# Multiply and tanh-GELU on one core: three DRAM stretches and two load queues, against two stretches and one

## The chip, the cores and the metric

The kernel runs on one core of a Trainium2 chip. The metric is device time in microseconds (us); the kernel before takes 119.77 us, the median of 3 runs that lie between 119.68 and 119.78.

A core has five instruction engines. Three matter here: VectorE (DVE in the profile) multiplies, ScalarE (ACT) applies the GELU, and SyncE (SP) issues DMAs and waits. Sixteen DMA engines carry all data between DRAM and the on-chip memory (SBUF, 128 partitions). A DMA becomes packets, here one packet for each row of a partition; the trace keeps a record of every packet with its queue, start, duration and size. Queue q1 is fed by SP, queue q10 by ACT.

## The reference

```python
def setup_inputs():
    batch, dim = 1024, 4096
    return {
        "x": np.random.randn(batch, dim).astype(np.float32),
        "y": np.random.randn(batch, dim).astype(np.float32),
    }

def reference(x, y):
    z = x * y
    return (0.5 * z * (1 + np.tanh(np.sqrt(2 / np.pi) * (z + 0.044715 * z ** 3)))).astype(np.float32)
```

Every element stands alone: 16.78 MB of x, 16.78 MB of y in, 16.78 MB out. Which element lies in which partition is therefore free, as long as x, y and the output agree.

## The kernel before, in words

The 4,194,304 elements are seen as 128 partitions of 32768 columns. `PIECES` (line 14) cuts the columns in three pieces: 1280, 16384 and 15104 columns. Each piece is one contiguous stretch of DRAM, and inside it partition p owns one contiguous row (`columns`, lines 51 to 55). The rows are 5120, 65536 and 60416 bytes long, and so are the packets. A DMA over 128 rows gives each of the 16 DMA engines 8 packets.

x has a place for all 32768 columns in SBUF (`xs`); the product and the GELU overwrite it, and the stores read it. y has a smaller buffer (`ys`, 20440 columns), so the second part of y can only be loaded when products have freed the room. `Y_LOADS` (line 16) lists y's loads as (first column, end, place in the buffer), and `Y_FREE` (line 18) how many products must be done before each is issued. The loads of y go in the order: middle piece (16384 columns), last piece (15104), first piece (1280).

The order of work is written out by hand:

- Two loads are hoisted ahead of the start-up barrier (`_hoist`): x's 1280-column piece on SP (line 79) and x's 16384-column piece on ACT (line 80). These two queues share the DMA engines at the opening.
- SP waits until the small piece of x has landed (line 81), then issues y's first load (line 82, issued by line 75) and x's last piece (line 83, issued by line 71).
- SP then waits for 3 products and issues y's second load, waits for the fourth and issues y's third (lines 84 to 87).
- DVE multiplies in steps (`STEPS`, line 20: four of 4096 columns; seven of 2048 and one of 768; one of 1280), each after the waits of lines 95 and 96. ACT follows each product with a GELU (line 107) after the wait of line 106.
- SP stores in three DMAs (lines 112 to 116): the middle piece after y's second load has fully landed (line 114), though its GELUs are done long before; then the last piece; then the small one. SP waits for the first two stores, clears the semaphores and waits for the third (lines 117 to 122).

All of SP's DMAs are on one queue, and on each DMA engine its packets go in the order in which they were issued.

Of the kernel before, what the change touches and what calls it, by code (L numbers as in the profile page):

```python
# [1 line left out]

# [4 lines left out]


F32 = mybir.dt.float32
GELU = mybir.ActivationFunctionType.Gelu_apprx_tanh  # L10

PIECES = [(0, 1280), (1280, 17664), (17664, 32768)]

Y_LOADS = [(1280, 17664, 4056), (17664, 32768, 0), (0, 1280, 15104)]

Y_FREE = [0, 3, 4]

STEPS = [[4096] * 4, [2048] * 7 + [768], [1280]]  # L20
STORES = [(1280, 17664), (17664, 32768), (0, 1280)]
Y_BUF = 20440


def _hoist(nc, issued):

    here = nc.cur_bb.bb.instructions
    first = nc.main_func.blocks[0].instructions
    for ins in issued:
        del here[next(k for k, i in enumerate(here) if i is ins or i.name == ins.name)]  # L30
    engine = issued[0].engine
    at = next(
        k
        for k, i in enumerate(first)
        if i.engine == engine and type(i).__name__ == "InstDrain"
    )
    first[at:at] = issued


@with_exitstack  # L40
def kernel(
    ctx: ExitStack,
    tc: tile.TileContext,
    x: bass.AP,
    y: bass.AP,
    out: bass.AP,
):
    nc = tc.nc
    P = nc.NUM_PARTITIONS

    def columns(t, a, b):

        flat = t.flatten_outer_dims().rearrange("r c -> (r c)")
        pa, pb = next(q for q in PIECES if q[0] <= a and b <= q[1])
        return flat[P * pa : P * pb].rearrange("(p c) -> p c", p=P)[:, a - pa : b - pa]


    tc.close()
    tc.compile()

    xs = nc.alloc_sbuf_tensor("xs", [P, PIECES[-1][1]], F32).ap()
    ys = nc.alloc_sbuf_tensor("ys", [P, Y_BUF], F32).ap()
    sem_x = [nc.alloc_semaphore(f"sem_x{i}") for i in range(len(PIECES))]
    sem_y = [nc.alloc_semaphore(f"sem_y{i}") for i in range(len(Y_LOADS))]
    sem_mul = nc.alloc_semaphore("sem_mul")
    sem_act = nc.alloc_semaphore("sem_act")
    sem_o = [nc.alloc_semaphore(f"sem_o{i}") for i in range(len(STORES))]

    def load_x(i, engine=nc.sync):
        a, b = PIECES[i]  # L70
        return engine.dma_start(out=xs[:, a:b], in_=columns(x, a, b)).then_inc(sem_x[i], 16)

    def load_y(i):
        a, b, r = Y_LOADS[i]
        return nc.sync.dma_start(
            out=ys[:, r : r + b - a], in_=columns(y, a, b)
        ).then_inc(sem_y[i], 16)

    _hoist(nc, [load_x(0).ins])
    _hoist(nc, [load_x(1, nc.scalar).ins])  # L80
    nc.sync.wait_ge(sem_x[0], 16)
    load_y(0)
    load_x(2)
    for i in range(1, len(Y_LOADS)):
        if Y_FREE[i]:
            nc.sync.wait_ge(sem_mul, Y_FREE[i])
        load_y(i)

    nc.scalar.wait_ge(sem_x[0], 16)
    n = 0  # L90
    done = {}
    for i, (a, b, r) in enumerate(Y_LOADS):
        for j, (xa, xb) in enumerate(PIECES):
            if xa <= a < xb:
                nc.vector.wait_ge(sem_x[j], 16)
        nc.vector.wait_ge(sem_y[i], 16)  # L96
        c = a
        for w in STEPS[i]:
            nc.vector.tensor_mul(  # L99
                out=xs[:, c : c + w],  # L100
                in0=xs[:, c : c + w],
                in1=ys[:, r + c - a : r + c - a + w],
            ).then_inc(sem_mul, 1)
            n += 1
            done[c + w] = n
            nc.scalar.wait_ge(sem_mul, n)
            nc.scalar.activation(  # L107
                out=xs[:, c : c + w], in_=xs[:, c : c + w], func=GELU
            ).then_inc(sem_act, 1)
            c += w  # L110

    for i, (a, b) in enumerate(STORES):
        if i == 0:
            nc.sync.wait_ge(sem_y[-2], 16)
        nc.sync.wait_ge(sem_act, done[b])
        nc.sync.dma_start(out=columns(out, a, b), in_=xs[:, a:b]).then_inc(sem_o[i], 16)
    for i in range(len(STORES) - 1):
        nc.sync.wait_ge(sem_o[i], 16)
    nums = sorted(s.num for s in [*sem_x, *sem_y, *sem_o[:-1], sem_mul, sem_act])
    assert nums == list(range(nums[0], nums[-1] + 1))  # L120
    nc.sync.sem_clear(range(nums[0], nums[-1] + 1))
    nc.sync.wait_ge(sem_o[-1], 16).then_inc(sem_o[-1], -16)


# [1 line left out]
_INS = ['x', 'y']  # L126
_OUTS = [((1024, 4096), 'float32')]


# [23 lines left out]
```

## Time and profile before

| what | value |
|---|---|
| runs of the kernel before | 119.68, 119.77, 119.78 us |
| profiled execution, first to last instruction (span) | 118.5 us |
| its first DMA packet starts, its last one ends | 1.01 us, 118.12 us |
| its last store has landed | 118.48 us |
| DVE busy, ACT busy | 35.2 us, 30.9 us |
| moved | 50.33 MB: 33.55 MB read, 16.78 MB written |

The profiled execution has no time of its own beside the span; the median of the runs stands 1.25 us above the span's 118.52 us. Times in the profile count from the first instruction, which is SP's hoisted DMA. "Busy" leaves out waits and DMA issues. "To landing" runs from a DMA's issue to the last increment of its semaphore; sixteen increments, one for each DMA engine, make a DMA complete.

### The profile page before, as it was taken

The page shows a single profiled execution, that of the slowest core. Times are in us where ns is not written, and L with a number is a line of the kernel's source. Part 1 is how long each engine was busy: PE and PEld are TensorE (multiplying, and loading weights), DVE is VectorE, ACT ScalarE, POOL GpSimd, SP SyncE. Part 2 cuts the span into 40 slices and gives each one's busy share as a digit, 9 for nine tenths or more (in the row PEclk, how much of TensorE's full clock was granted, in tenths as well). Part 3 has the DMA queues.
Part 4 walks back from the last instruction along what each step waited for, and adds up shares of the span by engine and source line. Part 5 has one row for each costly group of instructions (what it writes and reads, how often), then busy time and mean ns, then how long its engine had stood idle before and what let it go on. Part 6 is the DMA issues. An engine that isn't in the chain of part 4 may idle for free.

```text
span 118.5 us, 83 instructions
## 1 busy us (share of the span) xinstructions
DVE 35.2 (30%) x13; ACT 30.9 (26%) x14; POOL 0.2 (0%) x4
## 2 busy tenths in 40 slices
DVE  0000000000000069999920000059999940000000
ACT  0000000000000000999975000006998990000000
POOL 0000000000000000000000000000000000000000
DMA  9888899889988897798797797798899887977975
GB/s 492 382 382 382 354 597 464 354 354 465 597 354 354 354 632 347 326 632 347 326 632 347 326 632 347 326 575 354 354 531 531 354 354 326 653 326 326 653 326 221
DMA packets 1296, 50.33 MB, mean 425 GB/s; under 512 B 144, under 2 KB 144, under 8 KB 528
## 3 DMA queue, kind: packets, MB, share of 16 engines
q1 hardware_dynamic: 1152, 41.94, 82.3%
q10 hardware_dynamic: 144, 8.39, 16.5%
HBM read 33.55 MB, written 16.78 MB: 425 GB/s over the span
## 4 chain that ended last, share of the span: by engine, by line
DMA 55%; DVE 24%; ACT 3%; issue 1%; DVEq 0%
DMA ys<-in_y_dram 43%; DVE xs L99 24%; DMA xs<-in_x_dram 11%; ACT xs L107 3%; DVEq L96 0%
## 5 line engine op out<-in xcount | busy, mean ns | idle before, releaser
L99 DVE TENSOR_TENSOR xs<-xs,ys 128x2048 f32<-128x2048 f32 (+3 forms) x13 | 35.2, 2778 | 60.9 <-DMA ys<-in_y_dram 60.9
L107 ACT ACTIVATE xs<-xs 128x2048 f32<-128x2048 f32 (+3 forms) x13 | 29.6, 2300 | 19.6 <-DVE xs L99 19.6
L107 ACT ACT_TABLE_LOAD x1 | 1.3, 1283 | 47.2 <-DVE xs L99 47.2
L137 POOL MEMSET const-uint8-127<- 128x1 uint8 x1 | 0.1, 102 | 0.0
L137 POOL MEMSET const-bfloat16-1.0<- 128x1 bf16 x1 | 0.1, 101 | 0.0
L137 POOL MEMSET const-float32-0.0<- 128x1 f32 x1 | 0.1, 98 | 0.2 <-issue 0.2
L137 POOL MEMSET const-float32-1.0<- 128x1 f32 x1 | 0.1, 98 | 0.0
## 6 DMA issues: line engine op xcount, KB each, us to landing
xs<-in_x_dram SPq DMA_DIRECT2D x1, 7552.0 KB, 46.5
ys<-in_y_dram SPq DMA_DIRECT2D x1, 7552.0 KB, 22.5
out_dram<-xs SPq DMA_DIRECT2D x1, 7552.0 KB, 20.4
xs<-in_x_dram SPq DMA_DIRECT2D x1, 640.0 KB, 13.6
ys<-in_y_dram SPq DMA_DIRECT2D x1, 640.0 KB, 19.7
out_dram<-xs SPq DMA_DIRECT2D x1, 640.0 KB, 20.8
xs<-in_x_dram ACTq DMA_DIRECT2D x1, 30.4
ys<-in_y_dram SPq DMA_DIRECT2D x1, 29.0
```

The source lines that it names most:

```text
L99: nc.vector.tensor_mul(out=xs[:, c : c + w], in0=xs[:, c : c + w], in1=ys[:, r + c - a : r + c - a + w],).then_inc(sem_mul, 1)
L107: nc.scalar.activation(out=xs[:, c : c + w], in_=xs[:, c : c + w], func=GELU).then_inc(sem_act, 1)
L137: nc = _bacc.Bacc("TRN2", target_bir_lowering=False, num_devices=1)
```

## The change

The columns are cut in two stretches of 16384 columns, so that every row in DRAM is 65536 bytes, for x, y and the output. Only x's first half is hoisted, on SP; ACT issues no DMA. SP then issues y's first half and x's second half at once, without a wait. y's second half is still loaded in two parts, of 15104 columns (60416 bytes of each row, "59 KB") and 1280 columns (5120 bytes, "5 KB"), which are now parts of the same 65536-byte rows. Between them SP issues one load of 17 elements (68 bytes) into one partition, the marker, into a free place of y's buffer. The first store waits for the marker's semaphore instead of the whole 59 KB load. The products of the second half go 7 x 2048 columns, then the 1280 columns of the 5 KB load, then 384 and 384. There are two stores of 16384 columns each.

```diff
-PIECES = [(0, 1280), (1280, 17664), (17664, 32768)]
+PIECES = [(0, 16384), (16384, 32768)]
-Y_LOADS = [(1280, 17664, 4056), (17664, 32768, 0), (0, 1280, 15104)]
+Y_LOADS = [(0, 16384, 4056), (16384, 31488, 0), (31488, 32768, 15104)]
 Y_FREE = [0, 3, 4]
-STEPS = [[4096] * 4, [2048] * 7 + [768], [1280]]
-STORES = [(1280, 17664), (17664, 32768), (0, 1280)]
+STEPS = [(0, [(0, 4096), (4096, 4096), (8192, 4096), (12288, 4096)])] + [
+    (1, [(16384 + 2048 * k, 2048) for k in range(7)]),
+    (2, [(31488, 1280)]),
+    (1, [(30720, 384), (31104, 384)]),
+]
+STORES = PIECES
 Y_BUF = 20440
+MARK = 16384
...
     _hoist(nc, [load_x(0).ins])
-    _hoist(nc, [load_x(1, nc.scalar).ins])
-    nc.sync.wait_ge(sem_x[0], 16)
     load_y(0)
-    load_x(2)
+    load_x(1)
     for i in range(1, len(Y_LOADS)):
         if Y_FREE[i]:
             nc.sync.wait_ge(sem_mul, Y_FREE[i])
+        if i == len(Y_LOADS) - 1:
+            nc.sync.dma_start(
+                out=ys[0:1, MARK : MARK + 17], in_=columns(y, 0, 17)[0:1, :]
+            ).then_inc(sem_m, 16)
         load_y(i)
...
-    for i, (a, b, r) in enumerate(Y_LOADS):
-        for j, (xa, xb) in enumerate(PIECES):
-            if xa <= a < xb:
-                nc.vector.wait_ge(sem_x[j], 16)
-        nc.vector.wait_ge(sem_y[i], 16)
-        c = a
-        for w in STEPS[i]:
+    landed = set()
+    for i, steps in STEPS:
+        a, b, r = Y_LOADS[i]
+        j = next(j for j, (xa, xb) in enumerate(PIECES) if xa <= a < xb)
+        for key, sem in ((("x", j), sem_x[j]), (("y", i), sem_y[i])):
+            if key not in landed:
+                nc.vector.wait_ge(sem, 16)
+                landed.add(key)
+        for c, w in steps:
...
     for i, (a, b) in enumerate(STORES):
         if i == 0:
-            nc.sync.wait_ge(sem_y[-2], 16)
-        nc.sync.wait_ge(sem_act, done[b])
+            nc.sync.wait_ge(sem_m, 16)
+        nc.sync.wait_ge(sem_act, done[i])
         nc.sync.dma_start(out=columns(out, a, b), in_=xs[:, a:b]).then_inc(sem_o[i], 16)
```

More of the change, by code (lines that the diff above doesn't have):

```diff
@@ L64 @@
     sem_y = [nc.alloc_semaphore(f"sem_y{i}") for i in range(len(Y_LOADS))]
+    sem_m = nc.alloc_semaphore("sem_m")
     sem_mul = nc.alloc_semaphore("sem_mul")
@@ L104 @@
             n += 1
-            done[c + w] = n
+            done[j] = n
             nc.scalar.wait_ge(sem_mul, n)
@@ L109 @@
             ).then_inc(sem_act, 1)
-            c += w
     for i, (a, b) in enumerate(STORES):
         if i == 0:
-            nc.sync.wait_ge(sem_y[-2], 16)
-        nc.sync.wait_ge(sem_act, done[b])
+            nc.sync.wait_ge(sem_m, 16)
+        nc.sync.wait_ge(sem_act, done[i])
         nc.sync.dma_start(out=columns(out, a, b), in_=xs[:, a:b]).then_inc(sem_o[i], 16)
@@ L118 @@
         nc.sync.wait_ge(sem_o[i], 16)
-    nums = sorted(s.num for s in [*sem_x, *sem_y, *sem_o[:-1], sem_mul, sem_act])
+    nums = sorted(s.num for s in [*sem_x, *sem_y, *sem_o[:-1], sem_m, sem_mul, sem_act])
     assert nums == list(range(nums[0], nums[-1] + 1))
```

## The prediction

> **What bounds the kernel.** I read the busy row first, then the slices and the DMA queues, then SP's waits and the timeline, and last the packet records.
>
> ```profile
> DVE 35.2 (30%) x13; ACT 30.9 (26%) x14; POOL 0.2 (0%) x4
> ...
> DMA  9888899889988897798797797798899887977975
> ...
> q1 hardware_dynamic: 1152, 41.94, 82.3%
> q10 hardware_dynamic: 144, 8.39, 16.5%
> HBM read 33.55 MB, written 16.78 MB: 425 GB/s over the span
> ```
>
> No compute engine is busy for a third of the span; the two queues' packets fill 82.3 + 16.5 = 98.8% of sixteen engines' time. The DMA engines are the bound, and 1.2% (1.4 us) is all that better ordering can win. A stage in the middle shows what full means (the columns after the span are DVE, ACT and POOL busy, clock, DMA share, GB/s):
>
> ```profile
> 80.00:97.00 17.00, 16.12 (x9) 14.58 (x9) 0.00 (x0) 1.00 1.00 432
> ```
>
> A share of 1.00 moves 432 GB/s. So the question is where the packets do not run back to back. SP's waits and the timeline give the order:
>
> ```profile
> SPq L116 <- DMA ys<-in_y_dram: 14.5, 1, 14.5
> SPq L75 <- DMA xs<-in_x_dram: 12.1, 1, 12.1
> ...
> 0.00 0.38 SPq L71 DMA_DIRECT2D xs<-in_x_dram  x1
> 0.12 0.36 ACTq L71 DMA_DIRECT2D xs<-in_x_dram  x1
> ...
> 55.79 4.66 SPq L75 DMA_DIRECT2D ys<-in_y_dram  x2
> ...
> 78.27 19.77 SPq L116 DMA_DIRECT2D out_dram<-xs  x3
> 78.34 17.78 DVE L99 TENSOR_TENSOR xs<-xs,ys 128x2048 f32<-128x2048 f32 x9 [18.25 <-DMA ys<-in_y_dram]
> ...
> 93.88 3.80 ACT L107 ACTIVATE xs<-xs 128x2048 f32<-128x2048 f32 x3 [0.29 <-DVE xs L99]
> ```
>
> The last GELU ends at 97.69, 20 us before the end: stores alone fill the tail. From the packet records, start to start on one engine: a 64 KB load packet 2.4145 us, a 59 KB one 2.226, a 5 KB one 0.1915; a 64 KB store packet 2.42. Up to the end of the loads an engine owes 16 x 2.4145 + 16 x 2.226 + 16 x 0.1915 = 77.31 us. The sixteen finish them between 78.74 and 79.44, so 1.43 to 2.13 us went where no full-rate packet ran: 1.01 until the first packet, the rest nearly all in the opening. Summed over the engines, the mean loss behind the first packet is 0.47 us at 2.6 us, 0.63 at 6, and 0.72 at 78.5. In the opening, 5 KB packets that later take 0.196 take up to 0.756, and the first 64 KB packets of q10 up to 2.858 instead of 2.418. **The engine that is last never idles again**: its loads end at 79.44, then 38.68 us of store packets (19.32 + 17.81 + 1.55) end at 118.12, landing 0.36 later, at 118.48. The early engines wait from 78.74 to 79.11 for the first store and still end at 117.95. The time is the last engine's lag in the opening.
>
> **The change, part by part.**
>
> *Packets.* The same bytes: until the end of the loads an engine now owes 24 x 2.4145 + 8 x 2.226 + 8 x 0.1915 = 77.29 us, 0.02 less. The stores are 16 x 2.42 = 38.72 instead of 38.68. Nothing.
>
> *The opening.* SP's hoisted DMA stays the first instruction, with 64 KB rows; the 5 KB packets, ACT's DMA (0.36 us of ACT, which has nothing to do) and SP's 12.1 us wait go. That wait costs nothing today, since q10 keeps the engines full. SP issues two DMAs after the barrier, near 1.5 and 1.9 us, with 19 us of cover behind x's packets. The lag of the last engine is now: first packet at 1.01, as x's issue has it; spread over the engines 0.12, as when store 0 found idle engines (79.11 to 79.23); excess of a first 64 KB packet 0.44, the worst of q10's; later drift 0.07. Sum 1.64 against 2.13: with the 0.02, 0.51 us earlier. Both ends: with no excess and 0.05 spread, 1.13 and 1.0 us gained; with the old lag, nothing. I take 1.64, because q10's first packets are the same row length from the same tensor, and keep both ends.
>
> *y's second half.* The first products start after 1.64 + 16 x 2.4145 + 0.36 = 40.6; three of them take 13.1 (42.66 to 55.77), so the 59 KB load is issued near 53.8, while x's packets last to 59.6: 5.8 us of cover. The marker and the 5 KB load follow at 58.2; one more issue of 0.33 has 19 us of cover. If the queue took no more packets at once, SP would stand in that cover. The marker's own packet is bounded by a 4-byte completion packet (0.009) and a 5 KB one (0.196), on one place in the queue; I take 0.02, nearest the former, and only where the last engine carries it.
>
> *The wait of store 0.* Today it ends with the last of the sixteen increments (78.25; the first came at 77.67). Behind it on SP stand both stores. Between these ends I take the early one, less 0.5 from the opening; it can spare early engines the 0.37 us until 79.11. The last engine has 1.55 us of 5 KB packets to cover the 0.84 us from store issue to packet either way, so the end gets nothing. The Trainium skill (DMA: Bandwidth & Descriptors, section on why a DMA increments its semaphore by 16) says that 17 elements, a prime, go to a single DMA engine and that a later one-engine DMA says nothing of the other engines; no run here shows it yet, and by it the early end holds if that engine is an early one.
>
> *Store 1 waits for every GELU.* This is what is late next. Products before step by 2.20 us (2048 columns), 1.40 (1280), 0.87 (768): 0.066 + 1.04 ns a column, so 384 columns 0.47. GELUs step by 1.16 (1280) and 0.73 (768), so 384 columns 0.41. The seventh GELU ends at 95.80 on the old clock, then 1.16 + 0.41 + 0.41 gives 97.78 (products, done at 96.19, are ahead). That is 19.44 us after the first product, which moves 0.51 earlier: 97.27, store issued at 97.29, first packets 0.84 to 0.96 later, at 98.13 to 98.25. The last engine ends store 0 at 78.93 + 19.36 = 98.29. Cover of 0.04 to 0.16 us is left; without it every 0.1 us late is 0.1 us. Early engines idle up to half a microsecond there, free of charge as long as the last one doesn't. I add 0.05 for that margin and for store packets after an idle (2.454 instead of 2.42).
>
> *Sum.* 98.29 + 19.36 + 0.05 + 0.36 = 118.06 against 118.48 in the profile: 0.42 us less. The runs stand 1.25 us above the span, and I keep that: 119.77 - 0.42 = **119.35 us**.
>
> **The rivals.**
>
> *The opening gains nothing.* 16 engines start cold at one time, and the excess comes per byte or region, not per small packet. For it: the mean excess of x's 5 KB packets was 0.34 us per engine, of q10's first packets 0.17. Against it: the two add today. Time 119.55 to 119.95, middle 119.8.
>
> *The 64 KB load starts late; slower.* ACT's DMA was issued at 0.12, and its first packets came at 2.23 to 2.62. y's 64 KB load, issued at 13.57, was passed over at packet ends up to 15.64, 2.06 us after. If that is how long a 64 KB load takes to start, rather than a queue that was already serving another, the last engine's lag is 2.50 + 0.24 + 0.07 = 2.81, 0.68 more than today; with 0.05, 120.5. Against it: the 64 KB store had packets 0.84 us after its issue. It decides from a first packet at about 1.45 us (no gain) and is measurably slower from 1.7.
>
> *Store 1 late.* If a store's descriptors take longer than 0.96 us while other stores run, the margin is gone: 0.3 to 0.8 late gives 119.6 to 120.2. Against it: store 0 was issued beside running 5 KB packets.
>
> *Short rows at a 64 KB pitch.* The 5 KB load was contiguous and now takes 5 KB of every 64 KB. At the mean of the sixteen opening packets, 0.366, its eight cost 8 x 0.17 = 1.4 us more: 120.7 with the opening's gain. Against it: whole 64 KB rows run at 27.1 GB/s an engine, as the 59 KB ones do. The Trainium skill (DMA: Bandwidth & Descriptors, section on latency and other measured facts) has copies at row pitches of 4 MiB and 8 MiB falling to about half the rate, with aliasing of HBM channels as the inferred reason; here the 64 KB pitch shows no loss on long rows.
>
> **How the numbers follow.** Forecast 0.55, no gain in the opening 0.20, late start 0.12, store 1 late 0.08, short rows 0.05. A measurement of this kernel tells about 0.2% (0.24 us), so faster is below 119.53, slower above 120.01. The forecast's own range is 118.85 to 119.6, from the opening's bounds: 0.50 of it is faster, 0.05 the same. No gain gives 0.02 faster, 0.17 same, 0.01 slower; store 1 late 0.01 faster, 0.04 same, 0.03 slower; late start and short rows 0.17 slower. Together 0.53, 0.26, 0.21. Leaving out late start and short rows and 0.03 below, the range is 118.85 to 120.2.
>
> **What would show it.** In the changed profile: the first packet near 1.0 us and the sixteen y loads ending near 78.2 to 78.9 (opening; a first packet after 1.45 refutes it); the 5 KB packets at 0.196; the first store issued about 0.5 to 1 us before 78.27; the last GELU near 97.3; and no gap between the last engine's stores. If the end moves and the loads' end does not, the store side was wrong.

## The result and the profile after

The changed kernel takes 120.22 us (median of 4 runs, 120.15 to 120.32) against 119.78 us (119.68 to 119.79): a ratio of 1.0039, with a 95% interval of 1.0027 to 1.0051. It is 0.4% slower, a small difference that the runs still resolve, where 119.35 us was forecast. The profiled execution spans 118.98 us, 0.46 more than before's 118.52.

The page of the changed kernel, in the same rows as before:

```profile
DVE 35.3 (30%) x14; ACT 31.0 (26%) x15; POOL 0.2 (0%) x4
...
DMA  9889888998899888988897799798899888988888
...
q1 hardware_dynamic: 1010, 50.33, 98.5%
HBM read 33.55 MB, written 16.78 MB: 423 GB/s over the span
```

The DMA engines are still the bound: one queue fills 98.5% of their time, as the two filled 98.8%. The middle of the stores runs at the same full rate:

```profile
80.00:97.00 17.00, 16.59 (x10) 14.18 (x8) 0.00 (x0) 1.00 1.00 432
```

So the loss is again a matter of tenths in which an engine moves nothing. The timeline of the changed kernel shows by when it is there:

```profile
0.00 0.38 SPq L78 DMA_DIRECT2D xs<-in_x_dram  x1
...
1.43 0.33 SPq L82 DMA_DIRECT2D ys<-in_y_dram  x1
...
41.25 17.43 DVE L111 TENSOR_TENSOR xs<-xs,ys 128x4096 f32<-128x4096 f32 x4 [41.25 <-DMA ys<-in_y_dram]
...
54.38 0.33 SPq L82 DMA_DIRECT2D ys<-in_y_dram  x1
...
58.71 0.30 SPq L94 DMA_DIRECT2D ys<-in_y_dram  x1
...
78.44 20.11 SPq L127 DMA_DIRECT2D out_dram<-xs  x2
78.75 17.84 DVE L111 TENSOR_TENSOR xs<-xs,ys 128x2048 f32<-128x2048 f32 x10 [20.06 <-DMA ys<-in_y_dram]
...
94.28 3.90 ACT L119 ACTIVATE xs<-xs 128x2048 f32<-128x2048 f32 x4 [0.29 <-DVE xs L111]
```

Two numbers carry it. The first product starts at 41.25, where 40.6 was forecast. The first product of the second half starts at 78.75, where before it was 78.34 behind the same number of bytes: 0.41 us of the 0.46 are lost before the loads end. The first packets, from the packet records (start and duration in us), tell how:

```
changed kernel, 64 KB packets of x   before, 64 KB packets of q10 (five of sixteen each)
1.003  3.211                         2.229  2.847
1.019  3.267                         2.262  2.472
1.026  3.315                         2.358  2.719
1.737  2.474                         2.501  2.418
1.998  2.436                         2.620  2.662
(mean of all sixteen: 3.06)          (mean of all sixteen: 2.58)
```

The first packet comes at 1.00 us, on time; but the sixteen 64 KB packets take 0.64 us more than the 2.418 that they take later, the slowest 0.93 more. The engines also start less together than forecast: the sixteenth comes 1.00 us after the first, and the mean of all is 0.27 behind it. The 0.27 and the 0.64 make up the loss at 6 us that is used below. The same records show a second thing: the 59 KB load packets of y between 62 and 69 us took up to 2.436 instead of 2.229, a mean of 0.25 us per engine, and none did before. So there are two candidates for one loss.

### The profile page after: what moved, and what is told of

It is laid out like the page before. It is cut to its first block, busy times and chain, and to the rows that moved or that the text cites. A ratio compares the mean times of both kernels' runs of the same rounds, so it can differ in the third digit from the quotient of the medians.

```text
span 119.0 us, 82 instructions
## 1 busy us (share of the span) xinstructions
DVE 35.3 (30%) x14; ACT 31.0 (26%) x15; POOL 0.2 (0%) x4
## 3 DMA queue, kind: packets, MB, share of 16 engines
q1 hardware_dynamic: 1010, 50.33, 98.5%
## 4 chain that ended last, share of the span: by engine, by line
DMA 54%; DVE 24%; ACT 3%; issue 0%; DVEq 0%
DMA ys<-in_y_dram 54%; DVE xs L111 24%; ACT xs L119 3%; DVEq L108 0%
```

## The experiments

"Loss at 6 us" below is the mean loss that the prediction used: at 6 us, the time since the first packet, less what the packets so far cost at their full rate, averaged over the sixteen engines. It is 0.63 in the first profile of the kernel before and 0.92 in the changed kernel's. The last engine sets the end, so its own lag is given beside it: the time at which its last 64 KB packet of y's first half ends, less what its packets so far cost at their full rate.

Theory O puts the cost in the opening, theory P in y's 59 KB load with its new 64 KB pitch, theory S in the second store, which now waits for every GELU.

**after_again and before_again**: both kernels unchanged, for a second profile each.

> The changed kernel once more, unchanged, for a second profile of it. In the first one the 59 KB load packets of y between 62 and 69 us took up to 2.436 us instead of 2.229, a mean of 0.25 us per DMA engine and 0.33 for the last one. Theory P (the cost sits in y's 59 KB load because its rows are now parts of 64 KB rows): the stretched packets come again, at about the same place and size, span near 118.9. Theory O (the cost sits in the opening, where the first sixteen 64 KB packets took 2.44 to 3.35 us instead of 2.42): the first packets come out long again, whatever y's packets do; the stretch in y was a passing disturbance, and without it the loads end about 0.25 us earlier.

> The kernel before once more, unchanged, for a second profile of it. Both theories: span near 118.5, first 64 KB packets of the second queue up to 2.86 us, 59 KB load packets of y at 2.23. If here too some stretch of load packets is long by a few tenths, such a stretch is a passing disturbance and no effect of the row pitch.

after_again: 120.25 us, span 118.92, loss at 6 us 0.93, first packets 0.77 us over on the mean. The long 59 KB packets come again, but fewer: 12 of 128 over 2.26 us instead of 30, and 0.11 us per engine between 58 and 70 us instead of 0.25. before_again: 119.89 us, span 118.55, loss 0.69, no long 59 KB load packet. The opening repeats; the stretch in y is there again, at half its size, while the time is the same.

**open64**: the kernel before with the new opening alone.

```diff
-    _hoist(nc, [load_x(0).ins])
-    _hoist(nc, [load_x(1, nc.scalar).ins])
-    nc.sync.wait_ge(sem_x[0], 16)
+    _hoist(nc, [load_x(1).ins])
     load_y(0)
+    load_x(0)
     load_x(2)
...
-    nc.scalar.wait_ge(sem_x[0], 16)
+    nc.scalar.wait_ge(sem_x[1], 16)
```

> The kernel before with the new opening alone: x's 64 KB rows hoisted on SP, then y's 64 KB rows, then x's 5 KB and 59 KB pieces, all on SP and with no wait; ACT issues no DMA. Three stretches, three stores, no marker. Theory O (opening costs): first packets 2.4 to 3.35 us, mean loss 0.92 us behind the first packet instead of 0.63, time 120.0 to 120.2. Theory P (pitch of y's 59 KB load): 119.7 to 119.85. Theory S (the last GELU now gates the second store, which starts 0.05 to 0.16 us after engines are free): 119.7 to 119.85.

120.25 us, ratio 1.0036 (1.0022 to 1.0049): the whole loss, with old pieces, old stores and no marker. Loss at 6 us 0.93; no 59 KB packet over 2.26. Its DVE rows:

```profile
41.46 17.43 DVE L98 TENSOR_TENSOR xs<-xs,ys 128x4096 f32<-128x4096 f32 x4 [41.46 <-DMA ys<-in_y_dram]
78.72 17.77 DVE L98 TENSOR_TENSOR xs<-xs,ys 128x2048 f32<-128x2048 f32 x9 [19.83 <-DMA ys<-in_y_dram]
```

The second row starts at 78.72, as the changed kernel's 78.75, against 78.34 before.

**three**: the changed kernel with its second stretch cut in two again.

```diff
-PIECES = [(0, 16384), (16384, 32768)]
+PIECES = [(0, 16384), (16384, 31488), (31488, 32768)]
...
-    (1, [(16384 + 2048 * k, 2048) for k in range(7)]),
+    (1, [(16384 + 2048 * k, 2048) for k in range(7)] + [(30720, 768)]),
     (2, [(31488, 1280)]),
-    (1, [(30720, 384), (31104, 384)]),
...
     load_x(1)
+    load_x(2)
```

> The changed kernel with its second stretch cut in two again (columns 16384 to 31488 and 31488 to 32768), so that y's 59 KB and 5 KB loads are contiguous rows, with three stores and the products of the last piece last, as before; the new opening and the marker stay. Theory O: as open64, 120.0 to 120.2. Theory P: y's 59 KB packets at 2.229 throughout and 119.75 to 119.9. Theory S: the second store is issued a microsecond before it is needed, 0.05 to 0.1 us less than the changed kernel if that were all, 120.1 to 120.15.

120.24 us, ratio 1.0032 (1.0019 to 1.0045). y's 59 KB packets are all at their rate, the second store has a microsecond to spare, and the time is still the changed kernel's. So P and S fall as the cause: what they save together can't be told from nothing in the times. (In the profiled run the opening was a little worse than in the other profiles: loss at 6 us 0.99, the last engine's lag 2.40.) Between open64 and three lie, above all, the marker and the early first store: nothing either.

```profile
41.50 17.43 DVE L111 TENSOR_TENSOR xs<-xs,ys 128x4096 f32<-128x4096 f32 x4 [41.50 <-DMA ys<-in_y_dram]
78.77 17.77 DVE L111 TENSOR_TENSOR xs<-xs,ys 128x2048 f32<-128x2048 f32 x9 [19.84 <-DMA ys<-in_y_dram]
```

Now the question is what in the opening costs: one queue instead of two, the length of the packets, their pitch, or how far apart they lie.

**single5**: the kernel before with one queue.

```diff
-    _hoist(nc, [load_x(0).ins])
-    _hoist(nc, [load_x(1, nc.scalar).ins])
-    nc.sync.wait_ge(sem_x[0], 16)
+    _hoist(nc, [load_x(0).ins, load_x(1).ins])
```

> The kernel before with one queue: x's 5 KB rows and then its 64 KB rows are both hoisted on SP, ACT issues no DMA, and SP's wait for the small piece is gone. Theory L (a long packet that opens an idle engine is slow, a short one is not): the 5 KB packets open as before, mean loss near 0.6 us, 119.7 to 119.85. Theory Q (the second queue is what hides the start): mean loss near 0.9 us, 120.1 to 120.25.

119.81 us, ratio 0.9995 (0.9986 to 1.0003): one queue costs nothing, as long as 5 KB rows open it. Loss at 6 us 0.51, the last engine's lag 1.86 against 2.06 before.

```profile
0.00 0.85 SPq L71 DMA_DIRECT2D xs<-in_x_dram  x2
...
42.48 17.43 DVE L97 TENSOR_TENSOR xs<-xs,ys 128x4096 f32<-128x4096 f32 x4 [42.48 <-DMA ys<-in_y_dram]
78.24 17.77 DVE L97 TENSOR_TENSOR xs<-xs,ys 128x2048 f32<-128x2048 f32 x9 [18.34 <-DMA ys<-in_y_dram]
```

The second product row is back at 78.24. The Trainium skill (DMA: Bandwidth & Descriptors, section on issuing engines not being separate DMA queues) says that DMAs issued from several engines share the same sixteen DMA engines and gain only issue time; this pair of runs agrees.

**pitch5**: the changed kernel, with x's first half in two loads by columns, so that 5 KB packets open, but out of rows 64 KB apart.

```diff
+    X_LOADS = [(0, 1280), (1280, 16384), (16384, 32768)]
...
-        a, b = PIECES[i]
+        a, b = X_LOADS[i]
...
-    _hoist(nc, [load_x(0).ins])
+    _hoist(nc, [load_x(0).ins, load_x(1).ins])
     load_y(0)
-    load_x(1)
+    load_x(2)
...
```

> The changed kernel, except that x's first half is loaded in two hoisted DMAs on SP: columns 0 to 1280 (5 KB of every 64 KB row) and then columns 1280 to 16384 (59 KB of them). Theory L (length of the opening packet): short packets open, mean loss near 0.6, 0.25 to 0.35 us less than the changed kernel: 119.85 to 120.0. Theory A (the engines' first touch of sixteen places that lie 256 KB apart is slow, whatever the packet's length): the first 5 KB packets take about 0.9 us instead of 0.2, loss near 0.9, time as the changed kernel's, 120.15 to 120.3.

120.54 us, ratio 1.0055 (1.0041 to 1.0068), loss at 6 us 1.11. Short packets do not help: they take up to 1.396 us, and their excess over 0.196 sums to 0.72 us per engine, against 0.34 when the same sizes lie in one 0.66 MB stretch. Theory L falls as it stood. The sixteen 59 KB packets right behind them take 2.23: once the first ones are through, nothing is left of it. No 59 KB packet of y is long here either, though its pitch is 64 KB.

```profile
41.82 17.43 DVE L113 TENSOR_TENSOR xs<-xs,ys 128x4096 f32<-128x4096 f32 x4 [41.82 <-DMA ys<-in_y_dram]
78.98 17.84 DVE L113 TENSOR_TENSOR xs<-xs,ys 128x2048 f32<-128x2048 f32 x10 [19.74 <-DMA ys<-in_y_dram]
```

**warm**: the changed kernel, with 64 bytes of each row read first.

```diff
-    _hoist(nc, [load_x(0).ins])
+    warm = nc.sync.dma_start(out=ys[:, 0:16], in_=columns(x, 0, 16)).then_inc(sem_w, 16)
+    _hoist(nc, [warm.ins, load_x(0).ins])
...
```

> The changed kernel with one small load hoisted on SP ahead of x's first half: the first 16 columns (64 bytes) of each of its rows, into a free place of y's buffer, otherwise unused. Theory L: 8 short packets per engine do not move enough to cover a slow start of the long ones behind them, so the 64 KB packets still come out at about 3 us: 120.2 to 120.35. Theory A: the small packets touch the same places first and take the delay, while the 64 KB ones behind are already under way: first 64 KB packets at 2.4 to 2.6 us, and the time 0 to 0.3 us less than the changed kernel.

120.98 us, ratio 1.0087 (1.0073 to 1.0101). The 64-byte packets took 0.01 us each, and the 64 KB ones behind them still 2.76 to 3.59. A touch half a microsecond ahead pays for nothing, and pushes the start from 1.0 to 1.5. Theory A, in the form that the first touch of a place is slow, is not borne out.

**open59**: 59 KB rows in their own stretch open.

```diff
-Y_LOADS = [(1280, 17664, 4056), (17664, 32768, 0), (0, 1280, 15104)]
+Y_LOADS = [(17664, 32768, 5336), (1280, 17664, 0), (0, 1280, 16384)]
...
-STEPS = [[4096] * 4, [2048] * 7 + [768], [1280]]
-STORES = [(1280, 17664), (17664, 32768), (0, 1280)]
+STEPS = [[4096] * 3 + [2816], [2048] * 8, [1280]]
+STORES = [(17664, 32768), (1280, 17664), (0, 1280)]
...
-    _hoist(nc, [load_x(0).ins])
-    _hoist(nc, [load_x(1, nc.scalar).ins])
-    nc.sync.wait_ge(sem_x[0], 16)
+    _hoist(nc, [load_x(2).ins])
     load_y(0)
-    load_x(2)
+    load_x(0)
+    load_x(1)
...
```

> One look at an opening with 59 KB rows in a contiguous stretch (pitch 60416 bytes) in place of 64 KB rows at a 65536-byte pitch: x's 15104-column piece is hoisted on SP and worked on first, with its part of y. The order of the pieces is turned, so that the store of the middle piece becomes late by about 2 us, and its time is not read; only the opening is. Theory L: first sixteen packets about 0.7 us over their 2.23. Theory K (the engines run in step at a power-of-two distance): the 59 KB packets have 0.1 to 0.3 us over.

The first sixteen packets take 0.86 us over their 2.229, loss at 6 us 1.06 (and 122.25 us for the reason given). Theory K falls: the pitch need not be a power of two.

**w640, w2560, w5120**: single5 with the opening stretch at half, twice and four times the size. For w2560:

```diff
-PIECES = [(0, 1280), (1280, 17664), (17664, 32768)]
+PIECES = [(0, 2560), (2560, 18944), (18944, 32768)]
-Y_LOADS = [(1280, 17664, 4056), (17664, 32768, 0), (0, 1280, 15104)]
+Y_LOADS = [(2560, 18944, 4056), (18944, 32768, 0), (0, 2560, 13824)]
...
-STEPS = [[4096] * 4, [2048] * 7 + [768], [1280]]
-STORES = [(1280, 17664), (17664, 32768), (0, 1280)]
+STEPS = [[4096] * 4, [2048] * 6 + [1536], [2560]]
+STORES = [(2560, 18944), (18944, 32768), (0, 2560)]
```

> The one-queue kernel single5 with an opening stretch of 640 columns: 2.5 KB rows, 0.33 MB in all instead of 0.66. Theory A2 (what costs is how far apart in DRAM the sixteen engines' first packets lie, that is the size of the stretch that opens): mean loss behind the first packet at 6 us below single5's 0.51, 0.35 to 0.5, but the 64 KB rows now follow after 0.8 us and bring back some of it; 119.7 to 119.9. Theory G (short contiguous rows open well whatever the stretch's size, gaps or long packets open badly): 0.5 as in single5.

> The one-queue kernel with an opening stretch of 2560 columns: 10 KB rows, 1.31 MB. Theory A2: loss at 6 us between 0.55 and 0.75, 119.85 to 120.05. Theory G: 0.5, 119.75 to 119.85.

> The one-queue kernel with an opening stretch of 5120 columns: 20 KB rows, 2.62 MB. Theory A2: loss at 6 us between 0.65 and 0.85, 119.95 to 120.15. Theory G: 0.5 to 0.6, 119.8 to 119.9. The GELUs of the last piece are done with 10 us to spare in all three.

| opening stretch | rows | loss at 6 us | excess of its packets, per engine | last engine's lag | time |
|---|---|---|---|---|---|
| 0.33 MB (w640) | 2.5 KB | 0.73 | 0.39 | 1.98 | 120.80 |
| 0.66 MB (single5) | 5 KB | 0.51 | 0.34 | 1.86 | 119.81 |
| 0.66 MB (single5_mark, below) | 5 KB | 0.65 | 0.38 | 1.99 | 119.83 |
| 1.31 MB (w2560) | 10 KB | 0.92 | 0.65 | 2.10 | 120.52 |
| 2.62 MB (w5120) | 20 KB | 0.97 | 0.72 | 2.87 | 125.28 |
| 8.39 MB (open64) | 64 KB | 0.93 | 0.78 | 2.35 | 120.25 |

The openings first: between 0.66 and 1.31 MB the excess goes from 0.34 to 0.65, and beyond that it hardly grows. That is a step, not the slope that A2 expected, and theory G's 0.5 is refuted too. Two limits go with the table. Single5 and single5_mark open alike and still differ by 0.14 at 6 us, so w640 can't be told from them. And the loss and the excess are means over the engines: on the last engine, w2560's lag of 2.10 is close to the 2.06 of the kernel before, so its opening did not delay the end, and with one profile each it stays open where on that engine the price begins. The mean also flatters the short rows: between 6 and 58 us single5 and single5_mark lose another 0.22 us per engine, in 64 KB packets of up to 2.75 us, open64 only 0.04; no run here explains those packets.

The times missed all three expectations by other waits that I had not worked out. In w640 the last part of y is so short that it no longer covers the issue of the first store: 0.72 us per engine are lost between 78.4 and 80 us. In w2560 y's second load has long packets again, up to 0.47 us over, a mean of 0.38 us per engine between 58 and 70 us. In w5120 y's first half lands later while x's last piece is shorter, so y's second load is issued when the queue has run dry:

```profile
48.04 17.43 DVE L97 TENSOR_TENSOR xs<-xs,ys 128x4096 f32<-128x4096 f32 x4 [48.04 <-DMA ys<-in_y_dram]
...
61.16 4.67 SPq L75 DMA_DIRECT2D ys<-in_y_dram  x2
```

x's last packets end at 59.64 to 60.85 there, the load of y is issued at 61.16, and its first sixteen packets start at 62.14 to 62.71 and take 2.45 us on the mean instead of 1.665. That is a second opening in the middle of a kernel, after each engine had idled for more than a microsecond, and it costs 0.78 us over the rate as the first one does. So the price is not one of the program's start alone, though this is one case.

**single5_mark**: single5 with the marker.

```diff
...
+        if i == len(Y_LOADS) - 1:
+            nc.sync.dma_start(
+                out=ys[0:1, 16384 : 16384 + 17], in_=columns(y, 0, 17)[0:1, :]
+            ).then_inc(sem_m, 16)
...
-            nc.sync.wait_ge(sem_y[-2], 16)
+            nc.sync.wait_ge(sem_m, 16)
```

> The one-queue kernel single5 (1280 columns, 5 KB rows) with the marker load between y's 59 KB and 5 KB loads, and the first store waiting for it; three stores as before. If the last DMA engine alone sets the end, the early engines' idle time ahead of the first store (0.04 to 0.25 us on the mean) goes and the time stays: within 0.05 us of single5's. If engines share their rate, so that the mean counts, 0.1 to 0.2 us less than single5, and this beats the kernel before.

119.83 us, ratio 0.9996 (0.9987 to 1.0005). Loss between 78.4 and 80 us is 0.01 us per engine against single5's 0.05, so the early engines no longer wait; the time stays. The last engine sets the end, as the prediction had it. Neither this nor single5 can be told from the kernel before, so no version here beats it.

Two more runs are for the one thing still mixed: packet length and size of the stretch had changed together, except in pitch5.

**overlap**: open64, with 64 KB rows that start 5 KB apart.

```diff
+        src = columns(x, a, b)
+        if i == 1:
+            src = bass.AP(src.tensor, src.offset, [[1280, P], [1, b - a]])
-        return engine.dma_start(out=xs[:, a:b], in_=columns(x, a, b)).then_inc(sem_x[i], 16)
+        return engine.dma_start(out=xs[:, a:b], in_=src).then_inc(sem_x[i], 16)
```

> The kernel open64 with one edit: the 64 KB rows of the opening load start 5 KB apart in DRAM instead of 64 KB, so that they overlap and lie in 0.72 MB in all (x's values in that half are not the right ones; sizes and instructions are the same). Theory A2 (the size of the stretch that opens): first sixteen packets 0.3 to 0.4 us over 2.418, loss at 6 us near 0.55, 119.8 to 119.95. Theory L (packet length also counts): first packets 0.6 to 0.8 us over, loss near 0.9, 120.2 to 120.3 as open64.

120.15 us, ratio 1.0026 (1.0014 to 1.0039), loss at 6 us 0.82. The packets' excess falls to 0.39, as A2 said, but the sixteenth engine starts at 2.14 us instead of open64's 1.62, and most of the gain goes; the last engine's lag is 2.33, as open64's. The result lies between the two theories. The rows now read the same bytes from several engines at a time, which may have a price of its own.

```profile
78.67 17.77 DVE L101 TENSOR_TENSOR xs<-xs,ys 128x2048 f32<-128x2048 f32 x9 [19.85 <-DMA ys<-in_y_dram]
```

**gap10**: w2560, with 5 KB packets from rows 10 KB apart.

```diff
+    X_LOADS = [(0, 1280), (1280, 2560), *PIECES[1:]]
...
-        a, b = PIECES[i]
+        a, b = X_LOADS[i]
...
     _hoist(nc, [load_x(0).ins, load_x(1).ins])
-    load_y(0)
     load_x(2)
+    load_y(0)
+    load_x(3)
...
```

> The kernel w2560 with its opening load cut into two by columns: first 5 KB of every 10 KB row, then the other 5 KB, both hoisted on SP. The first 128 packets are as short as single5's but spread over 1.31 MB, with gaps. Read for the opening alone (w2560 loses time later, where a wait for products comes late). Theory A2: excess over 0.196 us summed per engine 0.55 to 0.75 us, as w2560's 0.65. Theory L: 0.34 to 0.38, as single5's.

The excess per engine is 1.01 us, more than w2560's 0.65 and three times single5's; the loss at 6 us is 1.20 (its one run took 122.30 us, which also holds other losses than the opening's). Packet length as the cause is refuted a second time, and A2's 0.55 to 0.75 is overshot.

**What is settled and what stays open.** Shown: the new opening alone makes a loss as large as the whole (open64), and the number of queues, the marker, the pitch of y's load and the merged store do not make it (single5, single5_mark, three). How the changed kernel's own loss divides is not shown. In its first profile the last engine's lag is only 0.1 us above the kernel before at the end of y's first half, and the long 59 KB packets add 0.33; in the second the two are 0.25 and 0.11. The four profiles of this opening (the changed kernel twice, open64, three) left the last engine anywhere from 2.15 to 2.40. Shown too: long rows, and short rows with gaps, lose more at 6 us than 5 KB rows that fill one 0.66 MB stretch, 0.82 to 1.20 against 0.51 to 0.69 in four profiles (warm's 1.5 holds its idle half microsecond too); 2.5 KB rows in 0.33 MB, at 0.73, can't be told from these. Why, inside the memory system, stays open: distance alone (overlap), length alone (pitch5, gap10), first touch (warm) and a power-of-two pitch (open59) were each tried and none explains all. Open too are the long packets of y's second load in the changed kernel, in warm (13 of them) and in w2560, but not in pitch5, which loads y as the changed kernel does.

## Why the prediction was wrong

- **What bounds the kernel**: right. DMA engines are the bound before and after, the last engine sets the end, and its lag comes from the opening, but for the long packets of y named below.
- **Packets**: right for all but y's 59 KB load, whose packets the prediction took at their old rate (below); 64 KB stores ran at 2.42 us.
- **The opening: this step failed.** The term was the "excess of a first 64 KB packet 0.44, the worst of q10's", in a lag of 1.64 us. Measured, the first sixteen packets are 0.64 to 0.78 us over on the mean and up to 1.14 for one packet (changed kernel twice, open64). The last engine's lag at the end of y's first half is 2.15 and 2.31 us in the changed kernel and 2.35 in open64, against 2.06 and 2.05 before: where I took 0.49 off, 0.1 to 0.3 was added. In the terms of the sum (first packet 1.01, spread 0.12, excess 0.44, drift 0.07), that engine had 1.00, 0.43, 0.70 and 0.02 in the first profile of the changed kernel and 1.03, 0.24, 1.04 and 0.01 in the second: the excess was mis-sized most, the spread over the engines too. The row for the excess was the wrong one: q10's first 64 KB packets came at 2.23 to 2.62 us to engines that had been reading for more than a microsecond; single5's, behind its 5 KB packets on one queue, are only 0.04 over. The lag that I wanted to remove, 5 KB packets of up to 0.756 us, belonged to one of the cheapest starts that any run here showed (loss at 6 us 0.63 and 0.69; the one-queue version of the same rows had 0.51 and 0.65).
- **y's second half**: the cover was there (y's load issued at 54.38, x's last packet at 60.1), the marker's packet took 0.012 us. Not foreseen were the long 59 KB packets, 0.33 us on the last engine in the first profile and 0.11 in the second; three lacks them and is no faster.
- **The wait of store 0**: right in its mechanism, not in its place. The marker's semaphore has two updates, one at 59.14, right behind its issue, and one at 78.42, between the first (78.10) and the last (78.65) landing of y's engines. That agrees with the Trainium skill (DMA: Bandwidth & Descriptors, section on why a DMA increments its semaphore by 16), by which a one-engine DMA has the other fifteen increments written at once. By then y's load had landed on twelve of the sixteen engines, so it was not the early end, as I had taken, and the store was issued at 78.44, not 0.5 to 1 us before the old 78.27. As worked out, the end got nothing from the marker.
- **Store 1**: right. From the first product of the second half to the last GELU 19.43 us (19.44 forecast), store issued at 98.20, first packets 0.85 to 1.00 later, the last engine free at 99.15 and idle for 0.05.
- **The rivals**: "the opening gains nothing" had the place but not the size, since it stopped at no gain; a loss there was foreseen only through a late first packet, and that came on time, at 1.00. The late start's break-even holds in another form: a start that is on time but slow does the same as a late one. Store 1 late and short rows at a 64 KB pitch did not come true: y's 5 KB packets all took 0.196.

## What to carry to other kernels

Where DMA engines run back to back to the end, the first microsecond is never made up, so price the opening from packets that met idle engines and not from the same packets behind others. Open with short rows that fill a small contiguous stretch, and queue the long rows right behind; one queue did that as well as two here. A gain for the early engines is worth nothing while the last one sets the end: follow the last one.

## What the runs showed of the hardware

- The first packets on idle engines: 64 KB load packets take 0.64 to 0.78 us more than their 2.418 on the mean, while 64 KB store packets on engines that had idled for up to half a microsecond took 2.457 on the mean (store 1 of the changed kernel), 0.04 over. Where they had idled for 1.7 to 2.0 us, ahead of open59's second store, the first sixteen took 2.478, 0.06 over: idleness alone does not make the price; here loads paid it and stores did not.
- An opening stretch of 0.66 MB costs its packets 0.34 to 0.38 us per engine on one queue, one of 1.31 MB 0.65, one of 8.39 MB 0.78: a step between the first two, in the mean over the engines. Engines that ran dry in mid-kernel pay again (w5120, 0.78).
- 5 KB of every 10 KB (1.01 us) opens worse than all of it (0.65), and 5 KB of every 64 KB costs 0.72; in steady state the same 5 KB packets out of 64 KB rows take 0.196.
